# A fused low-rank update on one core: narrow matmuls widened to the whole array, and the round's order changed

## The chip, the core and the metric

The kernel runs on one core of a Trainium2 chip. The metric is the device time of one execution in microseconds (us); before the change the median of three runs is 127.61 us. A core has TensorE (PE; its weight loads are shown as PEld), VectorE (DVE), ScalarE (ACT), GpSimd (POOL) and SyncE (SP), which here only issues transfers, and sixteen DMA engines that carry them.

## What is computed

```python
batch, seq, d_model, r = 16, 512, 768, 16
lora = np.matmul(np.matmul(x, A), B)
return (x + scale * lora).astype(np.float32)
```

x is 16 x 512 x 768 in float32, that is 8192 rows of 768, some 25 MB, read once and written once. A is 768 x 16, B is 16 x 768, scale is 0.5.

## The kernel before, in words

The 8192 rows are 64 tiles of 128 rows (NT), and four tiles (CHUNK) make a round, so there are 16 rounds (NC). All of x stays on the chip in one buffer, xs, and the result is added into it in place.

**Transfers.** SP issues all of them on one queue. Nine loads (LOADS: 2, 6, then seven times 8 tiles) go out first, with A and B after the second; the last load waits for "prep", since A and B are staged in the room that it fills. The stores follow in six parts (PARTS: 2, 6, 8, 16, 16, 16 tiles; in the order STORES: parts 2, 1, 0, 3, 4, 5). In a part of 16 tiles each partition holds 16 neighbouring rows of x, so its piece is one run of 49,152 bytes. Before a part that isn't yet known to be ready SP waits on the semaphore "added", which VectorE raises after a part's last addition with a drain (L185). Lines L130 to L137 are this loop.

**One round** goes over the engines like this:

- GpSimd converts x to float16, a round's four tiles by 256 columns at a time (`narrowed`, L94 to L106; three conversions a round, into xh; VectorE and ScalarE do two of the first round's). It waits for the load, and for the transposes of the round before to have read the buffer.
- TensorE transposes xh by matmuls with the identity (`turned(j)`, L202, four matmuls of 128 x 128 for each of six column blocks j) into PSUM, three buffers xt_ps.
- ScalarE copies each transposed block out as float16 (L160, into xt) and raises got j.
- TensorE projects: `projected(j)` (L213) has block j of A as its weights, 128 rows by 16 columns, streams xt of 512 columns, and accumulates over six j in yt_ps, 16 x 512.
- ScalarE scales yt_ps by 0.5 into yt (`scaled`, L153).
- TensorE expands: `expanded(s)` (L222) has 128 columns of yt, 16 rows, as weights and streams B, 512 and then 256 columns, into lo_ps, one of two PSUM buffers of 128 x 768.
- VectorE adds lo_ps to xs (L181), four times a round, and frees the buffer.

The engines' orders are written out by hand. TensorE's is staggered: a round's last projection, scaling and expansions run in the next round, among its transposes, so that every matmul finds its operand made. Before the change a round of the loop (L237 to L253) runs: transposes 0, projection 5 of the round before, transposes 1 and 2, expansion 0 (which waits for y), projection 0, transposes 3, expansion 1, projection 1, transposes 4, expansion 2, projection 2, transposes 5, expansion 3, projections 3 and 4. Waits on got, fed, freed and y keep data and buffers apart; TensorE itself lowers those semaphores again, in the `lowers` of `turned`.

ScalarE's order in a round: the eviction of transposes 0, then the scaling of the round before, then evictions 1 to 5 (L157 to L163).

**Before the rounds** GpSimd clears the staging rows of A and builds the identity (L109 to L115); VectorE converts its share of the first tiles, transposes A's staging rows into place, and converts A and B into a_mm and b_mm (L169 to L178), which raises "prep".

Of the kernel before, what the change touches and what calls it, by code (L numbers as in the profile page):

```python
# [9 lines left out]
MM_DT = mybir.dt.float16  # L10
# [7 lines left out]
CHUNK = 4  # L18
# [3 lines left out]
def kernel(  # L22
# [8 lines left out]
    nc = tc.nc  # L31
    fp32 = mybir.dt.float32
    add = mybir.AluOpType.add
    P = 128
# [3 lines left out]
    T, D = x2.shape  # L38
    R = A.shape[1]
    NT = T // P  # L40
    NC = NT // CHUNK
    ND = D // P
# [6 lines left out]
    sc = float(scale)  # L49

    sb = ctx.enter_context(tc.tile_pool(name="sb", bufs=1))
    ps = ctx.enter_context(tc.tile_pool(name="ps", bufs=1, space=bass.MemoryType.PSUM))

    xs = sb.tile([P, NT, D], fp32, name="xs")
    ident = sb.tile([P, P], MM_DT, name="ident")
    a_mm = sb.tile([P, ND, R], MM_DT, name="a_mm")
    b_mm = sb.tile([R, D], MM_DT, name="b_mm")
    xh = [sb.tile([P, CHUNK, W], MM_DT, name=f"xh{u}") for u in range(NU)]
    xt = [sb.tile([P, CHUNK * P], MM_DT, name=f"xt{j}") for j in range(ND)]
    first = sb.tile([P, 1], MM_DT, name="first")  # L60
    yt = sb.tile([R, CHUNK * P], MM_DT, name="yt")
    xt_ps = [ps.tile([P, CHUNK * P], fp32, name=f"xt_ps{b}") for b in range(NX)]
    yt_ps = ps.tile([R, CHUNK * P], fp32, name="yt_ps")
    lo_ps = [ps.tile([P, D], fp32, name=f"lo_ps{b}") for b in range(2)]


# [3 lines left out]
    b_f32 = xs[0:R, room + 2, :]  # L70
# [3 lines left out]
    def rows(t2, t0, n):  # L74
        i = max(i for i in range(len(PARTS)) if starts[i] <= t0)
        part = t2[ds(starts[i] * P, PARTS[i] * P), :].rearrange("(p s) d -> p s d", s=PARTS[i])
        return part[:, ds(t0 - starts[i], n), :]

    with tc.tile_critical():  # L79
# [3 lines left out]
        S = {k: nc.alloc_semaphore(name=f"s_{k}") for k in names}  # L83
# [10 lines left out]
        def narrowed(engine, c, u):  # L94
# [18 lines left out]
            out=ident, in_=ident, compare_op=mybir.AluOpType.not_equal, fill=1.0,  # L113
            base=0, pattern=[[-1, P]], channel_multiplier=1,
        ).then_inc(S["ident"], 1)  # L115


        load(0)
# [3 lines left out]
            out=a_rows[0:NB, :, :], in_=A.rearrange("(b a) r -> b a r", a=32)  # L122
# [7 lines left out]
        for i in STORES:  # L130
            t0, n = starts[i], PARTS[i]
            if i + 1 > summed_parts:
# [3 lines left out]
                out=rows(out2, t0, n), in_=xs[:, t0 : t0 + n, :]  # L136
# [14 lines left out]
        def scaled(c):  # L151
            nc.scalar.wait_ge(S["proj"], c + 1)
            nc.scalar.activation(  # L153
                out=yt, in_=yt_ps, func=mybir.ActivationFunctionType.Copy, scale=sc
            ).then_inc(S["y"], 1)

        for c in range(NC):  # L157
            for j in range(ND):
                nc.scalar.wait_ge(S["turned"], ND * c + j + 1)
                nc.scalar.copy(out=xt[j], in_=xt_ps[j % NX]).then_inc(S[f"got{j}"], 1)  # L160
                if j == 0 and c >= 1:
                    scaled(c - 1)
        scaled(NC - 1)  # L163


# [6 lines left out]
        nc.vector.transpose(out=a_t, in_=a_rows.rearrange("b a r -> b r a")).then_inc(S["a_t"], 1)  # L172
        nc.vector.wait_ge(S["a_t"], 1)
        a_tv = a_t[:, :, 0:NB].rearrange("a r (c k) -> a k c r", k=4)
        for k in range(4):
            nc.vector.tensor_copy(out=a_mm[ds(32 * k, 32), :, :], in_=a_tv[:, k, :, :])  # L176
        nc.vector.wait_ge(S["b"], 16)
        nc.vector.tensor_copy(out=b_mm, in_=b_f32).then_inc(S["prep"], 1)  # L178
        for k in range(NT):
            nc.vector.wait_ge(S["lora"], k + 1)  # L180
            nc.vector.tensor_tensor(  # L181
                out=xs[:, k, :], in0=xs[:, k, :], in1=lo_ps[k % 2], op=add
# [7 lines left out]
        def awaited(name, n=1):  # L190
            nc.tensor.wait_ge(S[name], n)

        def turned(j, waits={}, lowers={}):

            u, h = divmod(j, 2)
            waits, lowers = dict(waits), dict(lowers)
            if h == 0:
                waits[0], lowers[1] = f"fed{u}", f"fed{u}"
            for s in range(CHUNK):
                if s in waits:  # L200
                    awaited(waits[s])
                i = nc.tensor.matmul(  # L202
                    xt_ps[j % NX][:, ds(s * P, P)], xh[u][:, s, ds(h * P, P)], ident,
                    start=True, stop=True,
                )
                if s in lowers:
                    i.then_inc(S[lowers[s]], -1)
                if s == CHUNK - 1:
                    i.then_inc(S["turned"], 1)

        def projected(j):
            awaited(f"got{j}")
            i = nc.tensor.matmul(  # L213
                yt_ps, a_mm[:, j, :], xt[j], start=(j == 0), stop=(j == ND - 1)
            )
            if j == ND - 1:
                i.then_inc(S["proj"], 1)

        def expanded(s, name, n=1):
            awaited(name, n)  # L220
            for k, (n0, w) in enumerate(n_splits):
                i = nc.tensor.matmul(  # L222
                    lo_ps[s % 2][:, ds(n0, w)], yt[:, ds(s * P, P)], b_mm[:, ds(n0, w)],
                    start=True, stop=True,
                )
            i.then_inc(S["lora"], 1)
# [5 lines left out]
        for j in range(NX):  # L232
            projected(j)
            turned(NX + j, lowers={0: f"got{j}"})
        projected(3)
        projected(4)
        with nc.Fori(1, NC, engines=(mybir.EngineType.PE,)):  # L237
            turned(0, lowers={2: "got4"})
            projected(5)
            turned(1, lowers={0: "got5", 1: "got3", 2: "freed3"})  # L240
            turned(2, waits={3: "freed0"})
            expanded(0, "y")
            projected(0)
            turned(3, lowers={0: "got0", 1: "y", 2: "freed0"})
            expanded(1, "freed1")
            projected(1)
            turned(4, lowers={2: "got1"})
            expanded(2, "freed2")
            projected(2)
            turned(5, lowers={0: "got2", 1: "freed1", 2: "freed2"})  # L250
            expanded(3, "freed3")
            projected(3)
            projected(4)  # L253
# [41 lines left out]
```

## Time and profile before

| | |
|---|---|
| median of three runs | 127.61 us (127.55 to 133.83) |
| the profiled execution's own time | 127.5 us |
| its span, first to last instruction | 125.7 us |
| mean granted TensorE clock | 0.918 |
| busy: PE, PEld | 88.8 us, 36.4 us |
| busy: DVE, ACT, POOL | 64.0 us, 62.9 us, 49.9 us |
| moved by DMA | 50.46 MB, mean 401 GB/s |

The profile is one execution. Its page gives busy times by engine; a row of 40 slices for each engine, for the granted clock (tenths of full speed) and for the DMA engines; and groups of instructions by line, with their number, their mean length in ns and what ended the idle time before them ("<-"). Other views of the same trace list instructions in order of time (start, length, engine, line, operation, shapes, number merged), or give for a window of time each engine's busy time with its number of instructions, then granted clock, DMA share and GB/s. A matmul's length runs from its issue to its modelled end and overlaps that of the next one, so the distance from start to start says what it costs the array. "PEld" rows are weight loads. "SPq" is SP's queue of issues.

### The profile page before, as it was taken

The numbers are of one execution on the slowest core, as the hardware profiler recorded it, in microseconds if no ns is written. First come the engines' busy times: TensorE is split into PE (matmuls) and PEld (weight loads), VectorE is DVE, ScalarE is ACT, GpSimd is POOL, SyncE is SP. The second block draws the span as 40 slices with busy tenths as digits, with TensorE's granted clock in tenths as the row PEclk, the third lists the DMA queues.
The fourth block names the chain that finished last, engine by engine and source line by source line (L and its number), as shares of the span: only waits on it lengthen the run. The fifth ranks groups of instructions, "written<-read, shape, count | busy, mean of one in ns | idle before, by whom it ended". The sixth has DMA issues, their size and how long they took to land.

```text
span 125.7 us, 1582 instructions
## 1 busy us (share of the span) xinstructions
PE 88.8 (71%) x608; PEld 36.4 (29%) x608; DVE 64.0 (51%) x71; ACT 62.9 (50%) x115; POOL 49.9 (40%) x53
## 2 busy tenths in 40 slices
PE   0000799999999999999999999999999995200000
PEld 0000543433443343433443434434334431000000
DVE  0003606674858485675848494765848586500000
ACT  4003477667665847676675747576676651000000
POOL 3003566546456546456455556364464100000000
PEclk9999999999999999999999999999999997555555
DMA  3999999999999999999999999799989992559990
GB/s 117 438 428 409 391 469 407 446 414 446 430 399 477 391 461 409 438 422 446 407 407 403 431 407 561 344 500 438 469 347 485 454 438 125 250 250 500 500 500 0
DMA packets 2231, 50.46 MB, mean 401 GB/s; under 512 B 268, under 2 KB 268, under 8 KB 564
## 3 DMA queue, kind: packets, MB, share of 16 engines
q1 hardware_dynamic: 2228, 50.43, 94.4%
q14 instruction: 3, 0.02, 0.0%
HBM read 25.26 MB, written 25.17 MB: 401 GB/s over the span
## 4 chain that ended last, share of the span: by engine, by line
PE 58%; ACT 13%; DMA 8%; DVE 5%; issue 1%; SPq 0%; DVEq 0%
PE lo_ps L222 22%; PE yt_ps L213 19%; PE xt_ps L202 17%; DMA xs<-in_x_dram 8%; ACT xt L160 7%; ACT yt L153 6%; DVE xs L181 2%; DVE xs L172 1%; DVE a_mm L176 1%; DVE xh L105 1%; DVE b_mm L178 0%; SPq L90 0%; SPq L290 0%; DVEq L98 0%; SPq L79 0%
## 5 line engine op out<-in xcount | busy, mean ns | idle before, releaser
L181 DVE TENSOR_TENSOR xs<-xs,lo_ps 128x768 f32<-128x768 f32 x64 | 60.9, 954 | 33.2 <-PE lo_ps L222 28.0
L160 ACT CAST xt<-xt_ps 128x512 f16<-128x512 f32 x96 | 54.0, 580 | 30.9 <-PE xt_ps L202 30.9
L105 POOL CAST xh<-xs 128x1024 f16<-128x1024 f32 x46 | 48.7, 1059 | 47.1 <-PE xt_ps L202 37.8
L202 PE MATMUL xt_ps<-ident,xh 128*128 128x128 f16 x384 | 36.0, 225 | 13.1 <-POOL xh L105 13.1
L222 PE MATMUL lo_ps<-b_mm,yt 16*128 16x512 f16 (+1 forms) x128 | 32.2, 333 | 5.7 <-ACT yt L153 5.1
L213 PE MATMUL yt_ps<-xt,a_mm 128*16 128x512 f16 x96 | 34.3, 386 | 0.1
L202 PEld LDWEIGHTS xt_ps<-ident,xh 128*128 128x128 f16 x384 | 22.3, 99 | 34.2 <-issue 34.2
L213 PEld LDWEIGHTS yt_ps<-xt,a_mm 128*16 128x16 f16 x96 | 7.1, 86 | 21.6 <-issue 19.3
L222 PEld LDWEIGHTS lo_ps<-b_mm,yt 16*128 16x128 f16 x128 | 7.1, 93 | 14.7 <-ACT yt L153 6.9
L153 ACT ACTIVATE yt<-yt_ps 16x512 f16<-16x512 f32 x16 | 9.3, 582 | 0.6 <-PE yt_ps L213 0.6
L105 DVE CAST xh<-xs 128x1024 f16<-128x1024 f32 x1 | 0.7, 693 | 11.4 <-DMA xs<-in_x_dram 11.4
L103 ACT CAST xh<-xs 128x1024 f16<-128x1024 f32 x1 | 1.0, 1045 | 9.0 <-DMA xs<-in_x_dram 9.0
L148 ACT ACT_TABLE_LOAD x1 | 1.3, 1283 | 0.9 <-SPq L79 0.9
L172 DVE STREAM_TRANSPOSE xs<-xs 32x512 f32<-32x512 f32 x1 | 1.0, 1033 | 0.0
L176 DVE CAST a_mm<-xs 32x96 f16<-32x96 f32 x4 | 0.9, 231 | 0.1
L109 POOL MEMSET xs<- 32x512 f32 x1 | 0.5, 514 | 0.5 <-SPq L79 0.5
L178 DVE CAST b_mm<-xs 16x768 f16<-16x768 f32 x1 | 0.5, 549 | 0.0
L112 POOL TENSOR_SCALAR_AFFINE_SELECT ident<-ident 128x128 f16<-128x128 f16 x1 | 0.3, 292 | 0.2 <-POOL ident L110 0.2
L148 ACT COPY first<-ident 128x1 f16<-128x1 f16 x1 | 0.2, 194 | 0.0
L110 POOL MEMSET ident<- 128x128 f16 x1 | 0.2, 194 | 0.0
L276 POOL MEMSET const-float32-0.0<- 128x1 f32 x1 | 0.1, 99 | 0.2 <-issue 0.2
L276 POOL MEMSET const-bfloat16-1.0<- 128x1 bf16 x1 | 0.1, 101 | 0.0
(2 smaller groups left out, 0.2 us busy)
## 6 DMA issues: line engine op xcount, KB each, us to landing
xs<-in_x_dram SPq DMA_DIRECT2D x7, 3072.0 KB, 36.3
out_dram<-xs SPq DMA_DIRECT2D x3, 6144.0 KB, 20.8
out_dram<-xs SPq DMA_DIRECT2D x1, 3072.0 KB, 29.3
xs<-in_x_dram SPq DMA_DIRECT2D x1, 2304.0 KB, 9.9
out_dram<-xs SPq DMA_DIRECT2D x1, 2304.0 KB, 34.2
xs<-in_x_dram SPq DMA_DIRECT2D x1, 768.0 KB, 4.4
out_dram<-xs SPq DMA_DIRECT2D x1, 768.0 KB, 35.6
xs<-in_A_dram SPq DMA_DIRECT2D x1, 48.0 KB
```

The source lines that it names most:

```text
L103: i = engine.copy(out=xh[u], in_=src)
L105: i = engine.tensor_copy(out=xh[u], in_=src)
L109: nc.gpsimd.memset(a_rows, 0.0).then_inc(S["zeroed"], 1)
L148: nc.scalar.copy(out=first, in_=ident[:, 0:1])
L153: nc.scalar.activation(out=yt, in_=yt_ps, func=mybir.ActivationFunctionType.Copy, scale=sc).then_inc(S["y"], 1)
L160: nc.scalar.copy(out=xt[j], in_=xt_ps[j % NX]).then_inc(S[f"got{j}"], 1)
L172: nc.vector.transpose(out=a_t, in_=a_rows.rearrange("b a r -> b r a")).then_inc(S["a_t"], 1)
L176: nc.vector.tensor_copy(out=a_mm[ds(32 * k, 32), :, :], in_=a_tv[:, k, :, :])
L181: nc.vector.tensor_tensor(out=xs[:, k, :], in0=xs[:, k, :], in1=lo_ps[k % 2], op=add).then_inc(S[f"freed{(k + 2) % CHUNK}"], 1)
L202: i = nc.tensor.matmul(xt_ps[j % NX][:, ds(s * P, P)], xh[u][:, s, ds(h * P, P)], ident, start=True, stop=True,)
L213: i = nc.tensor.matmul(yt_ps, a_mm[:, j, :], xt[j], start=(j == 0), stop=(j == ND - 1))
L222: i = nc.tensor.matmul(lo_ps[s % 2][:, ds(n0, w)], yt[:, ds(s * P, P)], b_mm[:, ds(n0, w)], start=True, stop=True,)
```

## The change

The weights and the contraction of every matmul become 128 wide. a_mm has its six blocks of 16 columns side by side, followed by 112 zero columns, and a projection takes 128 columns from block j on: the first 16 rows of its output are y as before, the other 112 are not used. yt and b_mm get 128 rows, of which 16 hold data and the rest zeros. GpSimd clears the three buffers once, behind the identity, and VectorE waits for that before it writes A's blocks. In the order of a round projection 5 comes first, and expansion 1 follows expansion 0 directly, ahead of projection 0; ScalarE scales y before the round's first eviction. The prologue's and the epilogue's order on TensorE, the transfers and VectorE's additions are as they were.

```diff
-    a_mm = sb.tile([P, ND, R], MM_DT, name="a_mm")
-    b_mm = sb.tile([R, D], MM_DT, name="b_mm")
+    a_mm = sb.tile([P, ND * R + P - R], MM_DT, name="a_mm")
+    b_mm = sb.tile([P, D], MM_DT, name="b_mm")
-    yt = sb.tile([R, CHUNK * P], MM_DT, name="yt")
+    yt = sb.tile([P, CHUNK * P], MM_DT, name="yt")
-    yt_ps = ps.tile([R, CHUNK * P], fp32, name="yt_ps")
+    yt_ps = ps.tile([P, CHUNK * P], fp32, name="yt_ps")
...
+        nc.gpsimd.memset(a_mm, 0.0).then_inc(S["zeroed"], 1)
+        nc.gpsimd.memset(b_mm, 0.0).then_inc(S["zeroed"], 1)
+        nc.gpsimd.memset(yt, 0.0).then_inc(S["zeroed"], 1)
...
-                out=yt, in_=yt_ps, func=mybir.ActivationFunctionType.Copy, scale=sc
+                out=yt[0:R, :], in_=yt_ps[0:R, :], func=mybir.ActivationFunctionType.Copy, scale=sc
...
         for c in range(NC):
+            if c >= 1:
+                scaled(c - 1)
             for j in range(ND):
...
-                if j == 0 and c >= 1:
-                    scaled(c - 1)
...
+        nc.vector.wait_ge(S["zeroed"], 5)
         for k in range(4):
-            nc.vector.tensor_copy(out=a_mm[ds(32 * k, 32), :, :], in_=a_tv[:, k, :, :])
+            nc.vector.tensor_copy(
+                out=a_mm[ds(32 * k, 32), 0 : ND * R].rearrange("p (c r) -> p c r", r=R),
+                in_=a_tv[:, k, :, :],
+            )
         nc.vector.wait_ge(S["b"], 16)
-        nc.vector.tensor_copy(out=b_mm, in_=b_f32).then_inc(S["prep"], 1)
+        nc.vector.tensor_copy(out=b_mm[0:R, :], in_=b_f32).then_inc(S["prep"], 1)
...
-                yt_ps, a_mm[:, j, :], xt[j], start=(j == 0), stop=(j == ND - 1)
+                yt_ps, a_mm[:, ds(j * R, P)], xt[j], start=(j == 0), stop=(j == ND - 1)
...
         with nc.Fori(1, NC, engines=(mybir.EngineType.PE,)):
+            projected(5)
             turned(0, lowers={2: "got4"})
-            projected(5)
             turned(1, lowers={0: "got5", 1: "got3", 2: "freed3"})
             turned(2, waits={3: "freed0"})
             expanded(0, "y")
+            expanded(1, "freed1")
             projected(0)
             turned(3, lowers={0: "got0", 1: "y", 2: "freed0"})
-            expanded(1, "freed1")
             projected(1)
```

## The prediction

> **What bounds the kernel now.** I read the page first: how the span divides between TensorE and the DMA engines over time.
>
> ```profile
> span 125.7 us, 1582 instructions
> PEclk9999999999999999999999999999999997555555
> DMA  3999999999999999999999999799989992559990
> q1 hardware_dynamic: 2228, 50.43, 94.4%
> ```
>
> The DMA row stands at nine tenths from the second slice (3.1 us each) almost to the end: 50.43 MB pass, and the queue's packets fill 94.4% of sixteen engines' span. The one dent after the start is in slices 33 to 35, where the clock row also falls and compute ends. So two things can set the end: the transfers, or the compute that feeds the last store. The windows show which, around the dent.
>
> ```profile
> 64.00:103.00 39.00, 36.97 (x261) 15.25 (x261) 25.76 (x27) 26.07 (x49) 18.76 (x18) 1.00 1.01 435
> 103.50:104.00 0.50, 0.23 (x2) 0.00 (x0) 0.48 (x1) 0.23 (x1) 0.00 (x0) 1.00 2.27 983
> 104.00:104.50 0.50, 0.00 (x1) 0.03 (x2) 0.00 (x0) 0.35 (x1) 0.00 (x0) 1.00 1.36 590
> 104.50:105.00 0.50, 0.50 (x3) 0.27 (x4) 0.00 (x0) 0.00 (x0) 0.00 (x0) 1.00 0.00 0
> 105.00:105.50 0.50, 0.47 (x2) 0.00 (x0) 0.48 (x1) 0.00 (x0) 0.00 (x0) 0.50 0.24 98
> 106.00:106.50 0.50, 0.47 (x2) 0.12 (x2) 0.50 (x1) 0.00 (x0) 0.00 (x0) 0.50 0.00 0
> 109.00:109.50 0.50, 0.00 (x0) 0.00 (x0) 0.00 (x0) 0.00 (x0) 0.00 (x0) 0.50 0.00 0
> 109.50:110.00 0.50, 0.00 (x0) 0.00 (x0) 0.00 (x0) 0.00 (x0) 0.00 (x0) 0.50 3.70 1573
> 113.00:113.50 0.50, 0.00 (x0) 0.00 (x0) 0.00 (x0) 0.00 (x0) 0.00 (x0) 0.50 3.64 1573
> ```
>
> The last three columns are granted clock, DMA share and GB/s. A whole packet is counted in the window where it starts, so short windows count packets. In a part of 16 tiles each partition's piece is 16 x 768 x 4 = 49,152 bytes, one packet. 1573 GB/s over 0.5 us is 786 KB, sixteen of them, one for each engine; 983 is ten, 590 six, 98 one. Their length follows from the share: 2.27 x 0.5 x 16 / 10 = 1.82 us, and for the lone packet 0.24 x 0.5 x 16 = 1.92 us. So ten engines start their last packet of the part before at 103.5 to 104 and run dry by 105.8, six by 106.3, and one of the sixteen starts one more after 105.0 and ends near 107.2. Nothing starts until 109.5; then all sixteen begin the last store together. From 64 to 103 us the share is 1.01: no idle time at all.
>
> What the last store waits for stands in SP's own waits and its timeline:
>
> ```profile
> SPq L135 <- DVEq L185: 91.8, 4, 26.2
> ```
>
> ```profile
> 108.77 0.33 SPq L135 DMA_DIRECT2D out_dram<-xs  x1
> ```
>
> ```profile
> DMA to landing us min/median/max: 15.9/29.0/35.6
> ```
>
> SP sits before the stores until VectorE's drain says that a part has been added. It issues the last one at 108.77, which lands 15.9 later (the minimum: no queue ahead of it), at 124.7; the span ends 1.0 after that, and the profiled execution's 127.5 us are 1.8 more. The median stands at 127.61, so 0.1 above this execution. **The kernel is bound by transfers up to 105 us, and by compute for some 4 us after.** What a faster compute can win is that hole and no more.
>
> How the compute spends a round is in TensorE's timeline (rounds repeat; this one is 91.49 to 97.20, 5.71 us):
>
> ```profile
> 91.49 0.60 PE L213 MATMUL yt_ps<-xt,a_mm 128*16 128x512 f16 x2
> 92.02 0.40 PE L202 MATMUL xt_ps<-ident,xh 128*128 128x128 f16 x4
> 92.35 0.38 PE L213 MATMUL yt_ps<-xt,a_mm 128*16 128x512 f16 x1
> 92.66 0.62 PE L202 MATMUL xt_ps<-ident,xh 128*128 128x128 f16 x8
> 93.57 0.49 PE L222 MATMUL lo_ps<-b_mm,yt 16*128 16x512 f16 x2 [0.29 <-ACT yt L153]
> 94.00 0.38 PE L213 MATMUL yt_ps<-xt,a_mm 128*16 128x512 f16 x1
> 94.31 0.40 PE L202 MATMUL xt_ps<-ident,xh 128*128 128x128 f16 x4
> 94.64 0.49 PE L222 MATMUL lo_ps<-b_mm,yt 16*128 16x512 f16 x2
> ...
> 97.20 0.38 PE L213 MATMUL yt_ps<-xt,a_mm 128*16 128x512 f16 x1
> ```
>
> Starts tell more than lengths. A lone projection holds the array for 0.31 us (92.35 to 92.66, 94.00 to 94.31), but two in a row 0.53: the second adds 0.22. Four transposes alone hold it 0.33; four more of the same shape add 0.62 - 0.40 = 0.22. So each change from one kind of matmul to another costs about 0.1, and an expansion's 0.43 is 0.33 of work. A round has 14 changes. Work is 6 x 0.22 + 6 x 0.22 + 4 x 0.33 = 3.96; thirteen changes 1.3; and between the eight transposes (0.44) and the first expansion at 93.57 another 0.47, mostly the wait for scaled y, with the fourteenth change inside. Sum 5.73, against 5.71.
>
> **The change, part by part.** *The order.* A round now runs projection 5, transposes 0, 1, 2, expansions 0, 1, then as before. Kinds change 11 times instead of 14, which saves 0.3 at 0.1 each. And y is asked for at once: projection 5 starts the round, and ScalarE takes y ahead of the first eviction.
>
> ```profile
> L160 ACT CAST xt<-xt_ps 128x512 f16<-128x512 f32 x96 | 54.0, 580 | 30.9 <-PE xt_ps L202 30.9
> L153 ACT ACTIVATE yt<-yt_ps 16x512 f16<-16x512 f32 x16 | 9.3, 582 | 0.6 <-PE yt_ps L213 0.6
> L202 PEld LDWEIGHTS xt_ps<-ident,xh 128*128 128x128 f16 x384 | 22.3, 99 | 34.2 <-issue 34.2
> L213 PEld LDWEIGHTS yt_ps<-xt,a_mm 128*16 128x16 f16 x96 | 7.1, 86 | 21.6 <-issue 19.3
> ```
>
> ```profile
> 94.10 3.09 DVE L181 TENSOR_TENSOR xs<-xs,lo_ps 128x768 f32<-128x768 f32 x3 [1.55 <-PE lo_ps L222]
> ```
>
> Y is ready 0.38 (projection) + 0.58 (ScalarE) + some 0.1 of hand-overs = 1.06 after the round's start. Until then TensorE has 0.22 + 3 x 0.22 = 0.88 of work, or 1.08 if changes still cost 0.1. So the 0.47 becomes 0.1 to 0.2. The price is that evictions follow y: the first starts 0.5 later, and projection 0 now stands behind two expansions (0.66), by when it is there. The waits that the order moves stay covered: expansion 1 needs the buffer of the round's second to last add, and VectorE, at 3.09 / 3 = 1.03 each, needs 4.1 of a round.
>
> *The full array.* Projections load 128 columns instead of 16, expansions contract over 128 rows instead of 16 (the rows added are zero); counts and streamed columns stay. No row shows a projection of 128 columns. Bounds for its load: nothing, as for transposes (a fifth to eighth transpose adds 0.055 each though its 128-column load takes 0.099, so that load lies under other work), or the whole 0.099 bare, six times a round: 0.6. I take the first, by the same shape's row. And what of the 0.1 per change? If it comes from a change of shape, all of it goes; if from a change of operands, 11 remain. The rows can't tell, since shape and operand change together.
>
> The Trainium skill, page TensorEngine Tiling (Array Packing), section Tiling Modes, says that switching the tiling mode drains TensorE, while another tile of one mode does not; by that rule all 14 go and a round is 3.96 plus the wait for y. The trace agrees so far as every change here costs about 0.1.
>
> With all changes free the round is held by VectorE: y 1.06, first expansion done 0.49 later, two adds 2.06, then expansion 3 (0.33) and two projections (0.44): 4.4. With 11 left: 5.71 - 0.3 - 0.3 to 0.37, some 5.1. I take 4.4, as the 0.22 steps show matmuls of one shape in line without gaps.
>
> *The zeroing.* Three more memsets on GpSimd after the identity, for which VectorE waits before it writes A's blocks.
>
> ```profile
> 0.95 0.51 POOL L109 MEMSET xs<- 32x512 f32 x1 [0.50 <-SPq L79]
> 1.41 0.19 POOL L110 MEMSET ident<- 128x128 f16 x1
> 11.42 1.56 POOL L105 CAST xh<-xs 128x1024 f16<-128x1024 f32 x1 [9.30 <-DMA xs<-in_x_dram]
> ```
>
> Estimate: 512 columns took 0.51 and 128 took 0.19, so 208, 768 and 512 columns take some 0.3, 0.75 and 0.5, together 1.5. GpSimd is idle 9.30 until x lands at 11.4, and VectorE comes to A only after that landing: nothing, and 1.5 if that cover were gone (its own first cast and B's conversion, which releases SP's last load, would be late).
>
> *The sum.* Fifteen rounds at 4.4 instead of 5.71 bring the last store's issue forward 20 us, to 89. The hole needs far less: issued by 104.5 (0.8 before the engines run dry, as 108.77 to 109.6), that is 4.3 earlier, 0.28 a round. Even 5.1 gives 9. So compute stops to matter, and transfers run through to the end: each engine adds its eight packets of the last store to where it stood. The six late ones: 106.3 + 8 x 1.82 = 120.9, against 109.75 + 1.85 + 7 x 1.82 = 124.3. That is 3.4 less. The lone engine would end at 107.2 + 14.6 = 121.8, 2.5 less; its packets are 1.92 only while compute runs (all take 1.82 to 1.85 after 109.5). With compute over at 89 it is spared 0.1 on each of eight or nine packets, and ends with the others. I take 3.4: **127.5 - 3.4 = 124.1, as a median 124.2 us.** Bounds: 2.5 less if it lags as now (125.1), 1.9 if it stays at 1.92 to the end (125.7); 4.3 less if all sixteen ended like the first ten, at 105.4 + 14.6 (123.2).
>
> **The rivals.** *The lone engine sets the end*: 125.0 to 125.7, as just worked out. For it: it lags now, and queues are fixed before compute ends. Against: its slowness stops with compute.
>
> *The round is not shortened enough*: every load of 128 columns lies bare. Then 5.1 + 0.6 = 5.7, nothing is won, 127.5; half bare wins 0.3 a round and closes the hole. Against: the 0.055 of a transpose under a 0.099 load. The Trainium skill, TensorE: Matmul & The Clock Gate, section LDWEIGHTS (loading the stationary operand), speaks for it: load time goes with columns, P / 1.2, 13 ns for 16 and 107 for 128; by that the six would add 0.56 a round if bare. The trace disagrees on the first: 86 ns for 16 columns, 99 for 128.
>
> *Slower: the clock.* The granted clock is 1.00 until 105 and 0.50 after, in the tail where TensorE waits for VectorE. If the new waits inside a round (VectorE sets its pace) did that, work is 2 x 3.96 = 7.9 a round; from six such rounds of fifteen (6 x 7.9 + 9 x 4.4 = 87 against 15 x 5.71 = 85.7) the kernel is slower, and with all it is 15 x 2.2 = 33 later, 160. Against: TensorE waits 0.1 to 0.4 in a round of 4.4, and kept 1.00 with a wait of 0.29 in 5.71.
>
> **Chances.** Forecast (123.4 to 124.8) 0.75; lone engine 0.12; not enough 0.06 (125.7 to 127.6); clock 0.03; below 123.4, 0.04. Faster by over 2% (about what can be told from no change) is below 125.05: forecast, the case below it, and 0.05 of the lone engine's, 0.84. Within 2%: 0.13. Slower 0.03. The range reaches from the lower bound, 123.2, to the lone engine at its slowest, 125.7.
>
> **What would show it.** In the changed profile: no window without DMA packets between 12 us and the end; last store issued near 89, landing over 30 us later; rounds of 4.4 (or 5.1, which tells shape from operand and changes no time); 0.22 for lone projections; clock 1.00 to the end of the rounds. Wrong if the last store again meets an empty queue, or if packets get longer than 1.82 once compute is denser.

## The result, and the profile after

The changed kernel takes 124.4 us (median of six runs, 124.28 to 124.9); against the kernel before, run beside it, the ratio is 0.972, with a 95% interval of 0.969 to 0.976. Ratios here compare fast runs alone: of the six of the kernel before, five took 127.55 to 128.48 us, and one, at 133.83, fell into a slower state of the chip. The forecast was 124.2 us. The profiled execution took 124.9 us, at the upper end of the runs; its page begins:

```profile
span 123.1 us, 1586 instructions
PEclk9999999999999999999999999999755555555555
DMA  3999999999999999999999999999989979989970
q1 hardware_dynamic: 2228, 50.43, 96.3%
```

The dent in the DMA row is gone, and the clock row now falls at slice 28 instead of 33: compute ends earlier, while the same bytes pass. The queue's packets fill 96.3% of a shorter span.

SP's timeline has the last store's issue, and the view of that line of code the times to landing:

```profile
86.52 0.33 SPq L141 DMA_DIRECT2D out_dram<-xs  x1
```

```profile
DMA to landing us min/median/max: 35.5/39.3/42.1
```

The last store is issued 22 us earlier than before and lands 35.5 later (the minimum, at 122.05) instead of 15.9: it now stands in a queue. The windows of the changed kernel, with the same columns as before, over the place of the old hole and over the end:

```profile
64.00:86.00 22.00, 19.38 (x164) 11.20 (x161) 18.48 (x22) 15.20 (x30) 10.06 (x10) 1.00 1.03 442
104.50:106.00 1.50, 0.00 (x0) 0.00 (x0) 0.00 (x0) 0.00 (x0) 0.00 (x0) 0.50 0.99 426
106.00:109.50 3.50, 0.00 (x0) 0.00 (x0) 0.00 (x0) 0.00 (x0) 0.00 (x0) 0.50 1.01 435
118.50:119.00 0.50, 0.00 (x0) 0.00 (x0) 0.00 (x0) 0.00 (x0) 0.00 (x0) 0.50 0.91 393
119.00:119.50 0.50, 0.00 (x0) 0.00 (x0) 0.00 (x0) 0.00 (x0) 0.00 (x0) 0.50 0.23 98
119.50:120.00 0.50, 0.00 (x0) 0.00 (x0) 0.00 (x0) 0.00 (x0) 0.00 (x0) 0.50 0.24 98
120.00:120.50 0.50, 0.00 (x0) 0.00 (x0) 0.00 (x0) 0.00 (x0) 0.00 (x0) 0.50 0.00 0
```

The transfers have no hole from 104.5 to 109.5. At the end fourteen engines start their last packet by 119.0; two more packets start after that, one in each of the next two windows. Each is 0.5 us x 98 GB/s = 49,152 bytes. The trace has their starts, 119.41 and 119.90, and their length, 1.82 us, so two engines end late, at 121.2 and at 121.7, when the other fourteen are done by 120.6. The later one sets the end of this execution.

These are two different laggards, which shows when each is followed back through the trace, packet by packet. The one that ends at 121.2 is the slow engine of the prediction. Around 77.36 and 79.30 no other engine starts a packet of 49,152 bytes within 0.2 us, so small windows show its packets alone:

```profile
77.30:77.40 0.10, 0.10 (x5) 0.10 (x4) 0.10 (x1) 0.00 (x0) 0.10 (x1) 1.00 1.22 492
79.25:79.35 0.10, 0.10 (x3) 0.00 (x1) 0.10 (x1) 0.10 (x1) 0.00 (x0) 1.00 1.21 492
119.40:119.45 0.05, 0.00 (x0) 0.00 (x0) 0.00 (x0) 0.00 (x0) 0.00 (x0) 0.50 2.27 983
```

The first two are 1.22 x 0.1 x 16 = 1.95 and 1.94 us long, its last one 2.27 x 0.05 x 16 = 1.82. The engine that ends at 121.7 isn't slow: it ended the last load at 63.6, 1.1 us after the next engine, and each of its packets of 49,152 bytes takes 1.82. Why it fell behind is not shown. Without it this execution would have ended some 0.5 us earlier (121.7 - 121.2), which is near the median; the other executions were not traced.

A round on TensorE (transposes are L212, expansions L232, projections L223), from 60.26 on:

```profile
60.26 0.83 PE L212 MATMUL xt_ps<-ident,xh 128*128 128x128 f16 x12
61.10 0.82 PE L232 MATMUL lo_ps<-b_mm,yt 128*128 128x512 f16 x4
61.76 0.38 PE L223 MATMUL yt_ps<-xt,a_mm 128*128 128x512 f16 x1
61.98 0.39 PE L212 MATMUL xt_ps<-ident,xh 128*128 128x128 f16 x4
62.20 0.38 PE L223 MATMUL yt_ps<-xt,a_mm 128*128 128x512 f16 x1
62.42 0.39 PE L212 MATMUL xt_ps<-ident,xh 128*128 128x128 f16 x4
62.65 0.50 PE L232 MATMUL lo_ps<-b_mm,yt 128*128 128x512 f16 x2
62.99 0.38 PE L223 MATMUL yt_ps<-xt,a_mm 128*128 128x512 f16 x1
63.20 0.39 PE L212 MATMUL xt_ps<-ident,xh 128*128 128x128 f16 x4
63.52 0.50 PE L232 MATMUL lo_ps<-b_mm,yt 128*128 128x512 f16 x2
63.85 0.81 PE L223 MATMUL yt_ps<-xt,a_mm 128*128 128x512 f16 x3
```

A lone projection now holds the array for 0.22 us (61.76 to 61.98) and four transposes for 0.22 (61.98 to 62.20), as if no change of kind were there. The round takes 4.24 us instead of 5.71.

### The profile page after: what moved, and what is told of

It reads as the page before. It is cut to its first block, busy times and chain, and to the rows that moved or that the text cites. A ratio compares the mean times of both kernels' runs of the same rounds, so it can differ in the third digit from the quotient of the medians.

```text
span 123.1 us, 1586 instructions
## 1 busy us (share of the span) xinstructions
PE 69.8 (57%) x608; PEld 42.9 (35%) x608; DVE 60.0 (49%) x71; ACT 60.3 (49%) x115; POOL 51.1 (42%) x56
## 3 DMA queue, kind: packets, MB, share of 16 engines
q1 hardware_dynamic: 2228, 50.43, 96.3%
## 4 chain that ended last, share of the span: by engine, by line
PE 54%; DMA 8%; DVE 4%; ACT 1%; issue 1%; DVEq 1%; SPq 0%
PE lo_ps L232 20%; PE yt_ps L223 17%; PE xt_ps L212 17%; DMA xs<-in_x_dram 8%; DVE xs L191 2%; ACT xt L168 1%; DVE xs L178 1%; DVE a_mm L183 1%; DVEq L195 1%; ACT yt L159 0%; DVE b_mm L188 0%; SPq L93 0%; DVE xh L108 0%; SPq L300 0%; DVEq L101 0%
## 5 line engine op out<-in xcount | busy, mean ns | idle before, releaser
L191 DVE TENSOR_TENSOR xs<-xs,lo_ps 128x768 f32<-128x768 f32 x64 | 56.9, 950 | 14.9 <-PE lo_ps L232 14.7
L168 ACT CAST xt<-xt_ps 128x512 f16<-128x512 f32 x96 | 49.8, 578 | 4.1 <-PE xt_ps L212 1.7
L212 PE MATMUL xt_ps<-ident,xh 128*128 128x128 f16 x384 | 32.8, 223 | 13.2 <-POOL xh L108 13.2
L212 PEld LDWEIGHTS xt_ps<-ident,xh 128*128 128x128 f16 x384 | 27.6, 100 | 21.3 <-issue 13.7
L223 PE MATMUL yt_ps<-xt,a_mm 128*128 128x512 f16 x96 | 32.0, 384 | 0.2
L232 PE MATMUL lo_ps<-b_mm,yt 128*128 128x512 f16 (+1 forms) x128 | 29.1, 330 | 2.0 <-DVE xs L191 1.1
L223 PEld LDWEIGHTS yt_ps<-xt,a_mm 128*128 128x128 f16 x96 | 9.4, 98 | 11.3 <-ACT xt L168 5.4
L232 PEld LDWEIGHTS lo_ps<-b_mm,yt 128*128 128x128 f16 x128 | 8.6, 97 | 9.4 <-ACT yt L159 2.7
L120 POOL MEMSET b_mm<- 128x768 f16 x1 | 0.7, 738 | 0.0
L121 POOL MEMSET yt<- 128x512 f16 x1 | 0.5, 524 | 0.0
```

The source lines that it names most:

```text
L191: nc.vector.tensor_tensor(out=xs[:, k, :], in0=xs[:, k, :], in1=lo_ps[k % 2], op=add).then_inc(S[f"freed{(k + 2) % CHUNK}"], 1)
L212: i = nc.tensor.matmul(xt_ps[j % NX][:, ds(s * P, P)], xh[u][:, s, ds(h * P, P)], ident, start=True, stop=True,)
L223: i = nc.tensor.matmul(yt_ps, a_mm[:, ds(j * R, P)], xt[j], start=(j == 0), stop=(j == ND - 1))
L232: i = nc.tensor.matmul(lo_ps[s % 2][:, ds(n0, w)], yt[:, ds(s * P, P)], b_mm[:, ds(n0, w)], start=True, stop=True,)
```

## The experiments

**The theory**: the transfers set the end; compute has only to put the last store into the queue before the DMA engines run dry, near 105 us. If it does, its length is worth nothing more, except for the little that the one slow DMA engine adds while compute runs. **The rival**: the time follows the length of a round, so each part of the saving brings its part of the gain.

**The order alone.** Matmuls stay as before, 16 columns and 16 rows; TensorE's round and ScalarE's order are those of the change.

```diff
+            projected(5)
             turned(0, lowers={2: "got4"})
-            projected(5)
...
             expanded(0, "y")
+            expanded(1, "freed1")
```

> The order alone: matmuls as narrow as before, the round in the new order (projection 5 first, two expansions together, y scaled first). If the shape of a matmul makes the 0.1 us at each change, 11 of 14 changes keep it and a round takes 5.0 to 5.1 us, against 5.71 before and 4.24 in the changed kernel. Theory (the transfers set the end, and compute has only to put the last store into the queue before it runs dry): last store issued near 98 to 99 us, no hole in the transfers, 124.4 us, the same as the whole change within 0.5. Rival (the time follows the length of a round): 45% of the gain, about 126.4 us.

Measured: 124.8 us, ratio 0.974 (0.971 to 0.977). A round is 5.05, the last store is issued at 99.92. TensorE's timeline:

```profile
60.96 0.38 PE L213 MATMUL yt_ps<-xt,a_mm 128*16 128x512 f16 x1
61.28 0.40 PE L202 MATMUL xt_ps<-ident,xh 128*128 128x128 f16 x4
61.60 0.38 PE L213 MATMUL yt_ps<-xt,a_mm 128*16 128x512 f16 x1
```

A lone projection still takes 0.32. With less than half the saving in a round nearly all of the gain is there; the rival's 126.4 falls.

**The full array alone.** Buffers, weights and zeros as in the change, both orders as before; against the changed kernel:

```diff
-            projected(5)
             turned(0, lowers={2: "got4"})
+            projected(5)
...
             expanded(0, "y")
-            expanded(1, "freed1")
```

> The full array alone: 128 columns and 128 rows in every matmul, the round's order as before. No change of shape is left, so lone projections hold the array 0.22 us; but y is asked for later, after the first eviction, and a round takes 4.5 to 4.9 us by the wait for y and VectorE's additions behind it. Theory (transfers set the end): 124.4 us within 0.5. Rival (the time follows the round): 125.4 us. If the 0.1 us came from the change of operands and not of shape, a round would stay at 5.6 to 5.7 and the time at 127.5.

Measured: 124.68 us, ratio 0.973 (0.970 to 0.975). A round takes 4.72, last issue at 93.7:

```profile
60.15 0.38 PE L223 MATMUL yt_ps<-xt,a_mm 128*128 128x512 f16 x1
60.37 0.61 PE L212 MATMUL xt_ps<-ident,xh 128*128 128x128 f16 x8
61.47 0.50 PE L232 MATMUL lo_ps<-b_mm,yt 128*128 128x512 f16 x2 [0.49 <-ACT yt L159]
61.80 0.38 PE L223 MATMUL yt_ps<-xt,a_mm 128*128 128x512 f16 x1
62.02 0.39 PE L212 MATMUL xt_ps<-ident,xh 128*128 128x128 f16 x4
```

The operands change as often as before, and every lone projection takes 0.22: the 0.1 belonged to the change of shape. The wait for y is still there (0.49); with the new order 0.18 of it is left (shown below). Either half of the change brings the time down alone, and together they do not add.

**No faster compute at all.** The kernel before, with one edit to its stores:

```diff
-PARTS = [2, 6, 8, 16, 16, 16]
+PARTS = [2, 6, 8, 16, 16, 8, 8]
-STORES = [2, 1, 0, 3, 4, 5]
+STORES = [2, 1, 0, 3, 4, 5, 6]
```

> The kernel before, with its last part of 16 tiles stored as two of 8; compute is not touched, a round stays at 5.71 us and the last additions end near 108.7. Theory (the gain was the 4 us hole before the last store, nothing else): the first half goes into the queue near 97, keeps the engines fed until 112.7, the second half is queued by then, and the time falls to 124.4 to 125.2 with no faster compute at all; the one slow engine, slow as long as compute runs, keeps it at the upper end. Rival (faster compute is what gains): 127.5, unchanged.

Measured: 125.16 us, ratio 0.978 (0.974 to 0.983): a gain clear of the noise, though not clear of 2%. The timeline of SP, and the windows:

```profile
98.92 10.77 SPq L135 DMA_DIRECT2D out_dram<-xs  x2
```

```profile
106.00:109.50 3.50, 1.63 (x4) 0.25 (x4) 3.23 (x4) 0.00 (x0) 0.00 (x0) 0.55 1.01 435
```

Rounds stay at 5.71, the last additions end at 109.3, no earlier than before, and the hole is gone because the first half of the last part was in the queue at 98.92. The slow engine's packets take 1.9 until 103.5 here, and it ends last, at 121.8, 1.1 us after the next engine. This is the strongest of the tests: most of the gain comes from two lines that touch no matmul. The rival's 127.5 falls.

**The transfers alone.** Besides this edit the last load waits for A and B to land instead of "prep", and the work of the other engines on x is left out:

```diff
-                nc.sync.wait_ge(S["added"], summed_parts)
+                for k in sorted({part_of[s] for s in range(t0 + n)}):
+                    nc.sync.wait_ge(landed[k], 16)
```

> The transfers alone: the changed kernel without any compute (no conversions, transposes, projections, expansions, additions; x is stored as it was loaded); a part's store waits for its loads. Theory (the transfers set the end, and one DMA engine is slowed while compute runs): 123.2 to 123.7 us, the sixteen engines ending within 1 us of one another. If that engine's lag has nothing to do with compute: 124.4, the same as the changed kernel, one engine ending 1 us or more after the others. If compute still costs something in the changed kernel: 122 or less.

Measured: 123.82 us, ratio 0.966 (0.963 to 0.969). Windows of the end (without other engines only GpSimd's column stands ahead of clock, share and GB/s):

```profile
118.00:118.50 0.50, 0.00 (x0) 1.00 2.72 1180
118.50:119.00 0.50, 0.00 (x0) 1.00 0.45 197
119.00:119.50 0.50, 0.00 (x0) 1.00 0.00 0
```

All sixteen start their last packet before 119.0, and the engines end within 0.9 us of one another. No packet of 49,152 bytes takes longer than 1.82 us. So 123.82 is what these transfers cost with no compute, a little above the 123.2 to 123.7 expected, and the changed kernel stands 0.6 above it.

**Compute made longer, in two doses.** The first edit is both doses', the second (in the transposes, around their matmul) that of the larger alone; against the changed kernel:

```diff
-            for k, (n0, w) in enumerate(n_splits):
+            for k, (n0, w) in list(enumerate(n_splits)) * 2:
...
+                for again in range(2 if j < 3 else 1):
```

> The changed kernel with every expansion's two matmuls issued twice into the same buffer (the result is the same): 1.33 us more of TensorE in a round, less 0.17 of waits, about 5.4 us. Theory (transfers set the end until the last store misses the queue): last store issued at 103.5 to 105.5, just as the queue runs dry, 124.4 to 125.5 us. Rival (the time follows the round): 80% of the way back, near 127.

> As the dose before, and the transposes of column blocks 0 to 2 issued twice as well: 0.66 us more, a round near 5.95 us, longer than the 5.71 of the kernel before. Theory: the last store is issued near 112 and meets an empty queue, 130 to 132 us, so that past the knee each 0.1 us of a round costs 1.5 us. Rival (the time follows the round over its whole length): about 128.

Measured: the first dose has a round of 5.42, last issue at 104.88, and takes 125.45 us, ratio 0.978 (0.972 to 0.984). The second has a round of 5.91, last issue at 112.94, and takes 131.96, ratio 1.027 (1.021 to 1.033). In its windows the hole is back:

```profile
107.00:113.00 6.00, 3.67 (x19) 1.40 (x17) 4.54 (x5) 0.59 (x1) 0.00 (x0) 1.00 0.00 0
```

From 4.24 to 5.42 a round costs 1.1 us in all; the next 0.49 costs 6.5. That is the knee where the theory puts it, an issue near 105. The rival's 127 is too high for the first dose and its 128 too low for the second.

**Larger pieces.** The changed kernel with four parts of 16 tiles, A and B loaded behind the first; a second version has 8, 8, 16, 16, 16 for loads and stores.

```diff
-LOADS = [2, 6, 8, 8, 8, 8, 8, 8, 8]
+LOADS = [16, 16, 16, 16]
-PARTS = [2, 6, 8, 16, 16, 16]
+PARTS = [16, 16, 16, 16]
```

> The changed kernel with loads and stores in four parts of 16 tiles each, A and B behind the first: all packets are 49,152 bytes. The first conversion waits 6 us longer (17.5 instead of 11.4 us), and compute ends near 93. Theory (transfers set the end, compute has 16 us to spare): the late start costs nothing, and larger packets and fewer small ones save 1 us, 123.0 to 123.7. Rival (compute's end still counts): 130.

> The changed kernel with loads and stores of 8, 8, 16, 16, 16 tiles, A and B behind the first load. The first conversion starts as before (near 11.4 us). Theory: 123.3 to 124.2, between the changed kernel and the four parts of 16; no rival differs much here, this run is for the size of the gain.

Measured: 125.8 us, ratio 0.979 (0.974 to 0.984), and 124.78, ratio 0.971 (0.965 to 0.976). Both expectations missed: nothing was won, and the rival's 130 for the first missed too. The first eight engines end between 119.6 and 120.1 in both, as in the changed kernel, so the pieces' size hardly moves the sum. With parts of 16 the first conversion starts at 19.4 us and not at 17.5, and the packets that pass with A and B are slow:

```profile
17.00:18.00 1.00, 0.00 (x0) 0.00 (x0) 0.00 (x0) 0.00 (x0) 0.00 (x0) 1.00 1.88 623
```

623 KB are eleven packets of 49,152 bytes and 34 small pieces of A and B; in the trace the eleven take 2.3 to 2.5 us instead of 1.82. And compute ends at 95.1 instead of 86.4, and the slow engine ends last, at 122.1 (121.7 in the second version). That compute's late end costs through that engine fits; I did not separate it from the rest.

**The columns alone.** Against the changed kernel:

```diff
-    b_mm = sb.tile([P, D], MM_DT, name="b_mm")
+    b_mm = sb.tile([R, D], MM_DT, name="b_mm")
-    yt = sb.tile([P, CHUNK * P], MM_DT, name="yt")
+    yt = sb.tile([R, CHUNK * P], MM_DT, name="yt")
```

> The changed kernel with the columns widened only: projections load 128 columns, but yt and B keep their 16 rows in the expansions. If any difference of shape costs 0.1 us at a change, projections and transposes follow one another free (0.22 for a lone projection before transposes), and five changes a round to and from expansions still cost 0.1 each: a round of 4.4 to 4.8 us against 4.24. If only the narrow columns cost, a round stays at 4.24. The time by the theory (transfers set the end): 124.4 within 0.5 either way.

Measured: 124.58 us, ratio 0.970 (0.963 to 0.976), a round of 4.63.

```profile
61.67 0.39 PE L223 MATMUL yt_ps<-xt,a_mm 128*128 128x512 f16 x1
61.90 0.39 PE L212 MATMUL xt_ps<-ident,xh 128*128 128x128 f16 x4
62.12 0.38 PE L223 MATMUL yt_ps<-xt,a_mm 128*128 128x512 f16 x1
62.34 0.39 PE L212 MATMUL xt_ps<-ident,xh 128*128 128x128 f16 x4
62.66 0.49 PE L232 MATMUL lo_ps<-b_mm,yt 16*128 16x512 f16 x2
63.09 0.39 PE L223 MATMUL yt_ps<-xt,a_mm 128*128 128x512 f16 x1
```

Between projections and transposes a step is 0.22, as in the changed kernel. Transposes before an expansion take 0.32 (62.34 to 62.66) and the expansion 0.43, against 0.23 (62.42 to 62.65) and 0.34 there. So a change to fewer rows costs what a change to fewer columns does, about 0.1. A round has six such changes and is only 0.39 longer, as two of them fall into waits that the changed kernel has too: 0.18 before expansion 0, and 0.32 from the transposes at 63.20 to expansion 3.

**What slows the one DMA engine.** Two kernels put work beside the transfers alone: much of TensorE's, which touches nothing that is transferred, or the conversions of the three others.

```diff
+        with nc.Fori(0, 22, engines=(mybir.EngineType.PE,)):
+            for j in range(ND):
...
+                nc.tensor.matmul(yt_ps, ident, yt, start=True, stop=True)
```

```diff
+            for k in range(again):
...
+                    engine.tensor_copy(out=xh[u], in_=src).then_inc(S[f"fed{u}"], 1)
```

> The transfers alone, with TensorE kept busy beside them from 2 to some 90 us: 22 rounds of 38 matmuls on a buffer of zeros, which nothing waits for and which touch nothing that is transferred; no conversions, evictions or additions of the real work. If the one slow DMA engine is slowed by the number of instructions that execute (or that are recorded), its packets take 1.9 us again while this runs, it ends 1 us after the others, and the time is 124.3 to 124.6. If it is slowed by engines that read and write the buffers which the transfers use, nothing changes against the transfers alone: 123.8.

> The transfers alone, with the other three engines busy beside them from 11 to some 88 us: GpSimd, VectorE and ScalarE convert x's first four tiles again and again into xh (252 large instructions), TensorE does nothing. If the one DMA engine is slowed by the number of instructions, it is slowed little: 123.8 to 124.0 us. If it is slowed by the traffic of the other engines on the on-chip memory, its packets take 1.9 us while this runs, and the time is 124.3 to 124.6.

Measured: with TensorE's work 124.47 us, ratio 0.969 (0.964 to 0.974), and a packet starts late again:

```profile
64.00:86.00 22.00, 22.00 (x219) 15.27 (x217) 0.00 (x0) 1.00 1.03 442
119.00:119.50 0.50, 0.00 (x0) 0.00 (x0) 0.00 (x0) 0.50 0.23 98
```

With the conversions the time is 144.21, outside both expectations, and says nothing of the transfers: while GpSimd converts beside it, a conversion on VectorE takes 1407 ns instead of 693, so that its 108 ran on until 141.6. The transfers themselves were done at 121.1, and no packet of x starts after 119.0:

```profile
64.00:86.00 22.00, 21.45 (x17) 21.37 (x21) 21.05 (x16) 1.00 1.03 444
118.50:119.00 0.50, 0.50 (x1) 0.00 (x0) 0.00 (x0) 1.00 1.36 590
119.00:119.50 0.50, 0.47 (x2) 0.00 (x0) 0.00 (x0) 1.00 0.00 0
```

In 22 us the first ran 219 matmuls and 217 weight loads, the second 54 large instructions with three engines busy throughout. With the first, one engine's packets take 1.88 to 1.93 us from 77 to 92, where TensorE's work ends, and 1.82 after; it ends at 121.2, 0.7 after the next. With the second none of the 384 packets of 49,152 bytes takes over 1.86. So the lag comes with TensorE's many short instructions and not with the three other engines' traffic on the buffers, and TensorE's work alone brings the 0.6 by which the changed kernel stands above the transfers alone. Whether it is the number of instructions, TensorE's own work whatever the number, or the recording of so many in the trace stays open: no run here tells these apart.

## Why the prediction was right, point by point

*What bounds the kernel.* As read from the windows: transfers up to the hole, compute for the hole. Shown by the split last part (the hole closed with no faster compute), by the two doses (nearly flat up to an issue near 105, steep beyond) and by the transfers alone, 123.82.

*The order.* Y was to cost 0.1 to 0.2 of waiting; twelve transposes, at 0.22 for four, run from 60.26 to 60.92, and expansion 0 starts at 61.10, 0.18 later. The order alone gave 5.05 a round where "some 5.1" stood for the case that the changes of kind stay.

*The full array.* That shape and not operand makes the 0.1 was taken on a rule, as the rows couldn't tell: "The rows can't tell, since shape and operand change together." The full array alone decides it. The columns alone add that rows count as well. The page TensorEngine Tiling (Array Packing) of the Trainium skill, section Tiling Modes, says that changing the tiling mode drains the TensorE. These runs fit that, if matmuls of 16 columns or 16 rows are another mode than full ones: each change of shape costs 0.1 us, and none is left when all are 128x128. That the 0.1 is a drain no run shows.

*The wide loads.* None lies bare: three projections with 128 columns in a row take 0.81, so the second and third add 0.22 each (63.85), and a lone one holds the array for 0.22. The rival built on them is out.

*The round.* 4.4 forecast, 4.24 measured. The term that was mis-sized is VectorE's pace: 1.03 an addition was read from additions that waited for TensorE between them.

```profile
61.64 3.55 DVE L191 TENSOR_TENSOR xs<-xs,lo_ps 128x768 f32<-128x768 f32 x4 [0.69 <-PE lo_ps L232]
```

Four take 3.55, so 0.87 from start to start once they stand close. It changed next to nothing in the time, since a round's length hardly counts any longer; the last store went out at 86.5 instead of 89.

*The zeroing.* Three memsets of 0.27, 0.74 and 0.52, together the 1.5 estimated, all over by 3.5, with x landing at 11.4: nothing, as said.

*The slow DMA engine.* This step failed, though the time hardly shows it. The forecast spared this engine 0.1 us on each of eight or nine packets and let it end "with the others", so that six late engines set the end, at 120.9. Its packets do come down when compute ends: 1.94 and 1.93 us at 77.4 and 79.3, 1.83 to 1.85 from 81.2 to 86.7, and 1.82 from 88.6 on; TensorE's last round of the loop ends near 81.6. But it ends at 121.2, 0.6 us after the next engine; the other fourteen, of which six were to set the end, are done by 120.6, 0.3 earlier than summed. The sum took the engine's place in the queue from the profile before, where it began its first packet of 49,152 bytes at 77.0, 0.3 us ahead of the last engine. In the changed kernel's profile it began it at 77.4, 0.2 us behind the last of the fourteen. Why it stood later there is not shown. So the rival *the lone engine sets the end* had the mechanism right at too high a price (125.0 to 125.7), and a median within 0.2 us of the forecast is luck in part, since the errors of 0.6 and 0.3 partly cancel. In the profiled execution a third thing came on top, the engine that ended at 121.7 without being slow.

The lag gives a slight slope under the knee, not far above the spread of the runs. With a last store issued at 86.5, 93.2, 93.7 and 99.9 us the slow engine ends at 121.2, 121.3, 121.2 and 121.5, and the medians are 124.4, 124.58, 124.68 and 124.8. With no compute all engines end by 120.7, and the time is 123.82.

*The clock.* The granted clock is full until the rounds end (slice 28 of the page), so the slower rival had no occasion.

No version tried that computes the result beats the changed kernel; the one bound measured, the transfers alone, lies 0.6 below it. The changed kernel with its last part stored in two was not tried.

## What to carry to other kernels

When a store can't start before the last sum is done, look for the hole in front of it and cost a faster engine by that hole, not by its own saving: here 22 us of compute saved were worth 3.5, and two smaller last stores alone were worth most of that. Matmuls of different shapes in alternation cost TensorE 0.1 us at each change here; zeros up to the full array cost nothing in this kernel, where the streamed columns and the number of loads stay as they are. When transfers set the end, follow the last packet back to the engine that carries it, since the last engine isn't always the one that you expect. An interval read from an engine that waits is no pace for the same engine when it doesn't.

## What the runs showed that I had not expected

One DMA engine of sixteen takes 1.9 instead of 1.82 us for a stored packet of 49,152 bytes while seven to ten matmuls a microsecond run beside it, and 1.82 beside three other busy engines. The loads show no such engine: in the changed kernel, with compute running, the sixteen engines end three loads in a row within 25.05 to 25.66, 32.35 to 32.96 and 39.66 to 40.26 us, so none falls behind. VectorE and GpSimd, converting the same four tiles at the same time, take 1407 and 1378 ns instead of 693 and 1042 for each; once GpSimd is done, VectorE is back at 0.71 us.
